# Full-height products for the last 16 tokens, and one triangle product instead of two, in a two-layer hybrid kernel

## The chip, the cores and the metric

The kernel runs on one core of a Trainium2 chip. The metric is the device time of one execution in microseconds. Engines are named as in the profile: PE is the matrix engine (TensorE), PEld its weight loads, DVE the vector engine, ACT the scalar engine, POOL GpSimd, SP the engine that issues most transfers. "Lnnn" is a line of the kernel.

## The reference

A sequence of 256 frames, with 16 learned meta tokens ahead of it, passes two post-norm residual layers of width 2048. Layer 0 has two groups of heads behind one input projection: 4 heads of gated linear attention and 8 heads of stick-breaking attention. Layer 1 is a Mamba-2 mixer with 8 groups of 8 heads. Cut to the two parts that the change touches:

```
# layer 0, stick-breaking attention, per head (128 channels), block i of 128 queries
z         = q @ k.T                                  # keys up to the query's block
mask      = (key < query) & valid
log_stay  = where(mask, log_sigmoid(-z), 0)
within    = log_stay @ later_in_block                # strict triangle, per block of 128 keys
later     = sum of log_stay over the later key blocks
w         = where(mask, exp(log_sigmoid(z) + within + later), 0)
out       = w @ v

# layer 1, SSD scan, per head h of group g: y[t] = sum over s <= t of
#   exp(a_cum[t] - a_cum[s]) * (c[t] . b[s]) * dt[s] * x[s]   + d_skip * x[t]
```

## The kernel before

The 16 meta tokens and the 256 frames make 272 tokens, held with channels on the 128 rows and tokens along the columns. Over the tokens as rows, 272 is 128 + 128 + 16, so each token-by-token matrix comes in three blocks of keys: 128, 128 and the last 16 rows. Most of PE's work is projections: each unit of weights (128 x 2048) is loaded by SP, split by ACT (L159) and DVE or POOL (L160) into a high and a low part of type float32r, and multiplied in three passes (high by high, high by low, low by high: L178 to L180; L494 to L496 for the last projection). The token mixing of each head or group runs beside that: generators (`push`, `tick`) issue its steps between the products of the units. The order of the instructions on each engine is then laid out by the framework with a simulated timeline (`schedule_with_timeline_sim=True`); products marked with `keep_in_program_order` ("pin") stay in their own order, and the last stretches of both layers hold DVE and ACT in program order (`keep_order`).

**Layer 0, `mix_sb`.** The scores of one head lie in one bank of PSUM, `zb`, in 432 columns: 0 to 16 are the last 16 keys against the last 16 queries, 16 to 288 the first 128 keys against all 272 queries, 288 to 432 the second 128 keys against the last 144 queries. ACT, DVE and POOL make `sp` (softplus of the scores, masked) of it, and `parts_of` splits `sp` into `sph` and `spl`. The rows of the last 16 keys are copied into `sp2`, the high part into rows 0 to 15 and the low part into rows 32 to 47; the other rows of `sp2` hold zeros from the start of the kernel (L371 and L372). Then PE adds to `zb`: the negative triangle `nL_r` times both key blocks (L812 and L814), minus the sum of the second block onto the first (L816), minus the sum of the last 16 keys onto both blocks (L819: `nones_r[:48]` times `sp2`, 32 columns), and the triangle of the last 16 keys (L820: `nL2` times `sp2`, 16 columns out). ACT takes `zb` from there (L823). `sp2`, `nL2`, `sph`, `spl`, `nL_r` and `nones_r` are float32r. Here the trace calls `sph` and `spl` by their buffers, `s0h` and `s0l`.

**Layer 1, `mix_ssd`.** For a group, `M` holds the decayed token-by-token weights of 8 heads and `xd` the inputs times dt, with tokens as rows. L1257 multiplies them for the two blocks of 128 tokens; each head gives 64 rows of the output, so two heads stand side by side in the output's rows. For the last 16 tokens two heads share one product (L1263): `xd2` and `mt2` hold the one head in rows 0 to 15 and the other in rows 32 to 47, with zeros in between (memset at L936 and L937), and 32 columns, 16 for each. These tiles are plain float32; in the trace each product of that type makes two records. Both steps are pinned.

Of the kernel before, what the change touches and what calls it, by code (L numbers as in the profile page):

```python
# [6 lines left out]
F32 = mybir.dt.float32  # L7
F32R = mybir.dt.float32r
# [4 lines left out]
P = 128  # L13
# [69 lines left out]
def _wait(*tasks):  # L83
    for t in tasks:
        while not t.done:
            yield


class _Body:
# [181 lines left out]
    def layer0(self):  # L271
        nc, lp = self.nc, self.lp
# [37 lines left out]
        v2 = [lp.tile([80, 512], F32R, tag=f"v2{i}", name=f"v2{i}") for i in range(2)]  # L310
        s2 = [lp.tile([80, 1, 16], F32R, tag=f"s2{i}", name=f"s2{i}") for i in range(2)]
        self.v2, self.s2 = v2, s2
        self.sp2, self.nL2 = [lp.tile([48, n, 16], F32R, tag=t, name=t) for n, t in ((2, "sp2"), (1, "nL2"))]

        add4 = lp.tile([P, 432], F32, tag="ge", name="add4")[:, :P]

# [467 lines left out]
    def mix_sb(self, h, q, k, v):  # L784
        nc, lp = self.nc, self.lp
        act, vec, mm = nc.scalar.activation, nc.vector, nc.tensor.matmul
        zb = self.zbank()
        gk = dict(skip_group_check=True)

        for a, b in ((0, 0), (0, 1), (1, 0)):  # L790
            mm(zb[:, 16:288], k[:, a, 0:128], q[:, b, :], start=a == b, stop=False, **gk)
        for a, b in ((0, 0), (0, 1), (1, 0)):
            mm(zb[:, 288:432], k[:, a, 128:256], q[:, b, 128:T], start=False, stop=False, **gk)
        for a, b in ((0, 0), (0, 1), (1, 0)):
            mm(zb[:16, 0:16], k[:, a, 256:T], q[:, b, 256:T], start=False, stop=False, **gk)
        yield

        sp = e = lp.tile([P, 432], F32, tag="ge", name=self.nm("sbe"))
        act(e, zb[:, :432], AF.Abs)
        act(e, e, AF.Exp, scale=-1.0)  # L800
        act(e, e, AF.Ln, bias=self.b_one)
        vec.scalar_tensor_tensor(sp[:, :432], zb[:, :432], 0.0, e, op0=ALU.max, op1=ALU.add)
        yield
        self.causal(sp[:16, 0:16], 16, True)
        self.causal(sp[:, 16:144], 128, True)
        self.causal(sp[:, 288:416], 128, True)
        yield
        sph, spl = self.parts_of(sp, self.sp2, (0, 1))
        yield

        for s in (sph, spl):
            mm(zb[:, 16:288], self.nL_r, s[:, 16:288], start=False, stop=False, **gk)  # L812
        for s in (sph, spl):
            mm(zb[:, 288:432], self.nL_r, s[:, 288:432], start=False, stop=False, **gk)  # L814
        for s in (sph, spl):
            mm(zb[:, 144:288], self.nones_r, s[:, 288:432], start=False, stop=False, **gk)  # L816

        last = zb[:, 144:432].rearrange("p (a c) -> p a c", a=2)[:, :, 128:144]
        mm(last, self.nones_r[:48, :], self.sp2, start=False, stop=False, **gk)  # L819
        mm(zb[:16, 0:16], self.nL2[:, 0, :], self.sp2[:, 0, :], start=False, stop=True, **gk)  # L820
        yield
        w = self.spad
        act(w, zb[:, :432], AF.Exp)  # L823
        self.causal(w[:, 16:144], 128, True)
        self.causal(w[:, 288:416], 128, True)
        self.causal(w[:16, 0:16], 16, True)
        yield
        s2 = self.s2[h % 2]
        wh, wl = self.parts_of(w, s2, (0, 0, 1))
        yield  # L830
        while ("sv", h) not in self.tasks:
            yield
        yield from _wait(self.tasks["sv", h], self.tasks["sr", h // 4])
        o = self.po()
        self.values(o, *v, slice(0, P), wh, wl, s2)
        yield
        j, g = h % 4, 4 + h // 4
        mh, ml = self.mix_tile(g) if j == 0 else self.mix[g]
        y = lp.tile([P, T], F32, tag="gs2", name=self.nm("sby"), bufs=2)
        vec.tensor_tensor(y, o[:, :T], self.cur["sr", h // 4][:, j, :], op=ALU.mult)  # L840
        act(mh[:, j, :], y, AF.Copy)
        vec.tensor_tensor(ml[:, j, :], y, mh[:, j, :].bitcast(F32), op=ALU.subtract)
        yield
# [83 lines left out]
    def layer1(self):  # L927
        nc, lp = self.nc, self.lp
        self.acc = lp.tile([P, 2, D], F32, tag="acc", name="acc")
        self.y0 = self.y_tiles()  # L930
        self.mt = lp.tile([16, HPG, 16], F32, tag="mt", name="mt")


        self.mt2 = lp.tile([48, 4, 2, 16], F32, tag="mt2", name="mt2")
        self.xd2 = lp.tile([48, 4, 64], F32, tag="xd2", name="xd2")
        nc.vector.memset(self.mt2, 0.0)  # L936
        nc.vector.memset(self.xd2, 0.0)  # L937
        self.xq = lp.tile([P, 4, 32], F32, tag="xq", name="xq")
        nc.vector.memset(self.xq, 0.0)
        self.rstd1 = {}  # L940
        self.first1()
        self.units(len(L0), L1[:-5], {n: None for n in range(NFIRST)})
        self.tail()
# [537 lines left out]
```

## Time and profile before

| what | value |
|---|---|
| median of 3 runs | 1380.34 us (1380.31 to 1380.48) |
| profiled execution | 1380.1 us |
| its span, first to last instruction | 1378.4 us |
| PE busy | 1369.2 us (99%) |
| DVE busy | 1033.7 us (75%) |
| ACT busy | 770.1 us (56%) |
| POOL busy | 261.7 us (19%) |
| share of the 16 DMA engines, main queue | 53.8% |
| granted PE clock over the span | 0.999 |
| stick-breaking heads, L812 to L820 | 438 to 631 us of the span |
| groups of layer 1, L1257 and L1263 | 776 to 1309 us of the span |

Products are pipelined: the duration of one in the trace is from its start to a modelled end, and the next one starts before that. So PE's pace is read from start to start. A form such as "48*128 48x32" is weights of 48 rows by 128 columns and a moving operand of 48 rows by 32 columns; float32r stands as f32 in the forms of PE.

### The profile page before, as it was taken

To read this page: it belongs to the slowest core of one execution; us is meant where nothing else is said; L and a number is where in the kernel's file an instruction comes from. 1 tells how busy PE (TensorE), PEld (TensorE's weight loads), DVE (VectorE), ACT (ScalarE), POOL (GpSimd) and SP (SyncE) were. 2 spreads that over 40 slices of the span, in tenths; PEclk is the share of its full clock that TensorE was granted. 3 is DMA by queue.
4 is the path that set the end of the run, shared out by engine and by line. 5 is a ranking of instruction groups with operands and counts; after the bars stand their busy time and mean duration, and the time that the engine had idled before them with its cause. 6 is when DMAs were issued, how large, how long until landed. Compare 5 with 4: busy or idle time off the path is not lost.

```text
span 1378.4 us, 26195 instructions
## 1 busy us (share of the span) xinstructions
PE 1369.2 (99%) x10619; PEld 1319.5 (96%) x10619; DVE 1033.7 (75%) x1763; ACT 770.1 (56%) x1149; POOL 261.7 (19%) x253
## 2 busy tenths in 40 slices
PE   9999999999999999999999999999999999999998
PEld 8999999999999999999999999899898999989986
DVE  7858576576565574568899999887877879777687
ACT  6646455355345554556587677656565655656551
POOL 0000010100101100004500143331322323133221
PEclk9999999999999999999999999999999999999999
DMA  9656446446445455554455655565555555555561
GB/s 333 207 173 200 166 162 209 160 163 217 168 158 188 139 192 167 196 168 136 136 196 170 240 203 203 177 240 184 210 176 202 185 200 217 172 194 186 183 214 62
DMA packets 61945, 256.73 MB, mean 186 GB/s; under 512 B 26176, under 2 KB 29056, under 8 KB 33408
## 3 DMA queue, kind: packets, MB, share of 16 engines
q1 hardware_dynamic: 61104, 254.27, 53.8%
q8 instruction: 83, 1.36, 0.4%
q10 hardware_dynamic: 720, 0.79, 0.2%
q14 instruction: 38, 0.31, 0.1%
HBM read 249.29 MB, written 5.74 MB: 185 GB/s over the span
## 4 chain that ended last, share of the span: by engine, by line
PE 92%; DVE 5%; issue 1%; DMA 1%; POOL 0%; ACT 0%; SPq 0%; ACTq 0%; DVEq 0%; POOLq 0%
PE pj L178 25%; PE pj L179 25%; PE pj L180 25%; PE pj L494 4%; PE pj L496 4%; PE pj L495 4%; PE po L1257 1%; PE po L631 1%; DVE wlo L160 1%; DVE M L1127 1%; DMA raw<-in_wts 0%; PE po L1196 0%; DVE M L1128 0%; DVE M L1155 0%; DVE xt L1072 0%
## 5 line engine op out<-in xcount | busy, mean ns | idle before, releaser
L178 PE MATMUL pj<-xhi,whi 128*128 128x272 f32 (+4 forms) x2560 | 731.6, 286 | 1.5 <-ACT xhi L330 0.6
L179 PE MATMUL pj<-xlo,whi 128*128 128x272 f32 (+4 forms) x2560 | 730.4, 286 | 0.0
L180 PE MATMUL pj<-xhi,wlo 128*128 128x272 f32 (+4 forms) x2560 | 729.7, 285 | 0.0
L159 ACT ACTIVATE whi<-raw 128x1024 fp32r<-128x1024 f32 (+2 forms) x434 | 449.2, 1038 | 384.0 <-PE pj L179 312.3
L160 DVE TENSOR_TENSOR wlo<-raw,whi 128x1024 fp32r<-128x1024 f32 (+2 forms) x405 | 503.1, 1247 | 200.4 <-ACT whi L159 192.6
L178 PEld LDWEIGHTS pj<-xhi,whi 128*128 128x128 f32 x2560 | 482.0, 188 | 3.7 <-ACT whi L159 1.3
L179 PEld LDWEIGHTS pj<-xlo,whi 128*128 128x128 f32 x2560 | 482.0, 188 | 1.7 <-issue 1.0
L180 PEld LDWEIGHTS pj<-xhi,wlo 128*128 128x128 f32 x2560 | 482.1, 188 | 0.4 <-issue 0.4
L178 PE MATMUL pj<-mixh,whi 128*128 128x272 f32 x384 | 110.7, 290 | 0.0
L180 PE MATMUL pj<-mixh,wlo 128*128 128x272 f32 x384 | 110.5, 288 | 0.0
L179 PE MATMUL pj<-mixl,whi 128*128 128x272 f32 x384 | 110.4, 288 | 0.0
L160 POOL TENSOR_TENSOR wlo<-raw,whi 128x1024 fp32r<-128x1024 f32 x29 | 73.1, 2522 | 191.2 <-ACT whi L159 176.7
L494 PE MATMUL pj<-whi,yh 128*128 128x512 f32 (+1 forms) x240 | 93.3, 389 | 0.0
L495 PE MATMUL pj<-wlo,yh 128*128 128x512 f32 (+1 forms) x240 | 92.6, 386 | 0.0
L496 PE MATMUL pj<-whi,yl 128*128 128x512 f32 (+1 forms) x240 | 92.2, 386 | 0.0
L261 POOL TENSOR_TENSOR gr<-gr,gsc 128x1088 f32<-128x1088 f32 x6 | 15.4, 2575 | 303.1 <-ACT gsc L260 303.1
L179 PEld LDWEIGHTS pj<-mixl,whi 128*128 128x128 f32 x384 | 72.3, 188 | 0.2
L180 PEld LDWEIGHTS pj<-mixh,wlo 128*128 128x128 f32 x384 | 72.3, 188 | 0.0
L178 PEld LDWEIGHTS pj<-mixh,whi 128*128 128x128 f32 x384 | 72.2, 188 | 0.2
L503 DVE SCALAR_TENSOR_TENSOR acc<-pj,rr,acc 128x512 f32<-128x512 f32 (+1 forms) x65 | 46.5, 734 | 13.9 <-PE pj L496 13.7
L496 PEld LDWEIGHTS pj<-whi,yl 128*128 128x128 f32 x240 | 45.1, 188 | 9.2
L494 PEld LDWEIGHTS pj<-whi,yh 128*128 128x128 f32 x240 | 45.1, 188 | 8.9
(349 smaller groups left out, 1460.5 us busy)
## 6 DMA issues: line engine op xcount, KB each, us to landing
raw<-in_wts SPq DMA_DIRECT2D x212, 1024.0 KB, 4.9
ebc<-edr SPq DMA_DIRECT2D x8, 1664.0 KB, 6.5
raw<-in_wts SPq DMA_DIRECT2D x9, 256.0 KB, 5.4
vdr<-vt SPq DMA_DIRECT2D x8, 256.0 KB, 4.8
vt<-vdr SPq DMA_DIRECT2D x32, 64.0 KB, 2.4
hacc<-in_xT SPq DMA_DIRECT2D x7, 272.0 KB, 6.1
early<-in_wts SPq DMA_DIRECT2D x2, 512.0 KB, 7.1
vdr<-vt SPq DMA_DIRECT2D x8, 128.0 KB, 3.5
```

The lines of the kernel that those rows point to most:

```text
L159: self.nc.scalar.activation(hi, src, AF.Copy)
L160: eng.tensor_tensor(lo, src, hi.bitcast(F32), op=ALU.subtract)
L178: mm(ps, whi, xhi, start=first, stop=False)
L179: mm(ps, whi, xlo, start=False, stop=False)
L180: mm(ps, wlo, xhi, start=False, stop=last)
L261: mul(c, c, e, op=ALU.mult)
L494: mm(ps, yh[:, kk, tt], hi[:, k, :], start=kk == 0, stop=False)
L495: mm(ps, yh[:, kk, tt], lo[:, k, :], start=False, stop=False)
L496: mm(ps, yl[:, kk, tt], hi[:, k, :], start=False, stop=kk == 3)
L503: self.nc.vector.scalar_tensor_tensor(a, ps, r[:, t : t + 1], a, op0=ALU.mult, op1=ALU.add)
L631: mm = lambda r, a, b, start=False, stop=False: self.nc.tensor.matmul(o[:, r], a, b, start=start, stop=stop, skip_group_check=True)
L1127: vec.tensor_scalar(M[:, h, 0:256], eb[:, h, 0:256], self.est[:, 0, 0, gh : gh + 1], 0.0, op0=ALU.subtract, op1=ALU.min)
```

## The change

The tiles with the last 16 tokens get 128 rows instead of 48, so that the zeros go on to row 127 and the products over them contract over 128 rows. The instructions that fill them are the same, with more rows. L812 takes both key blocks at once, columns 16 to 432, and the two products of L814 are gone.

```diff
@@ layer0
-        self.sp2, self.nL2 = [lp.tile([48, n, 16], F32R, tag=t, name=t) for n, t in ((2, "sp2"), (1, "nL2"))]
+        self.sp2, self.nL2 = [lp.tile([P, n, 16], F32R, tag=t, name=t) for n, t in ((2, "sp2"), (1, "nL2"))]
@@ mix_sb
         for s in (sph, spl):
-            mm(zb[:, 16:288], self.nL_r, s[:, 16:288], start=False, stop=False, **gk)
-        for s in (sph, spl):
-            mm(zb[:, 288:432], self.nL_r, s[:, 288:432], start=False, stop=False, **gk)
+            mm(zb[:, 16:432], self.nL_r, s[:, 16:432], start=False, stop=False, **gk)
         for s in (sph, spl):
             mm(zb[:, 144:288], self.nones_r, s[:, 288:432], start=False, stop=False, **gk)
 
         last = zb[:, 144:432].rearrange("p (a c) -> p a c", a=2)[:, :, 128:144]
-        mm(last, self.nones_r[:48, :], self.sp2, start=False, stop=False, **gk)
+        mm(last, self.nones_r, self.sp2, start=False, stop=False, **gk)
         mm(zb[:16, 0:16], self.nL2[:, 0, :], self.sp2[:, 0, :], start=False, stop=True, **gk)
@@ layer1
-        self.mt2 = lp.tile([48, 4, 2, 16], F32, tag="mt2", name="mt2")
-        self.xd2 = lp.tile([48, 4, 64], F32, tag="xd2", name="xd2")
+        self.mt2 = lp.tile([P, 4, 2, 16], F32, tag="mt2", name="mt2")
+        self.xd2 = lp.tile([P, 4, 64], F32, tag="xd2", name="xd2")
```

The line numbers behind the change are two lower from L814 on.

## The prediction

> **What bounds the kernel now.** First the head of the page and its chain line.
>
> ```profile
> span 1378.4 us, 26195 instructions
> ...
> PE 92%; DVE 5%; issue 1%; DMA 1%; POOL 0%; ACT 0%; SPq 0%; ACTq 0%; DVEq 0%; POOLq 0%
> ```
>
> The chain of work that ended last is TensorE for 92%, so a product that goes away counts unless something is late right behind it. Since the change has two places, one in layer 0 and one in layer 1, I next asked for the busy time by stretches (columns: stretch, length, then PE, weight load, DVE, ACT, POOL, granted clock, DMA).
>
> ```profile
> 420.00:722.00 302.00, 302.00 (x2438) 300.58 (x2437) 209.78 (x357) 168.19 (x275) 49.54 (x77) 1.00 0.51 169
> 722.00:842.00 120.00, 118.57 (x995) 113.48 (x994) 117.63 (x227) 86.83 (x138) 33.63 (x27) 1.00 0.58 209
> 842.00:1330.00 488.00, 488.00 (x3635) 457.65 (x3634) 378.41 (x587) 287.54 (x409) 138.14 (x104) 1.00 0.55 194
> ```
>
> The reader sees three regimes. From 420 to 722 (the stick-breaking heads and the end of layer 0) TensorE is never idle. From 842 to 1330 (layer 1, groups 2 to 7) neither. Between them, VectorE is busy 117.63 of 120 and TensorE idles 1.43: there VectorE holds part of the chain. The waits and the chain of that stretch name the place:
>
> ```profile
> PE pj L178 <- DVE fix L958: 0.5, 1, 0.5
> ...
> 722.42 0.45 PE po L1012 x4
> 722.93 0.43 DVE xlo L984
> ...
> 724.10 1.14 DVE wlo L160
> ```
>
> Up to 722.42 the chain is TensorE's own, and VectorE's run from 722.93 starts off it. So time taken out of TensorE in layer 0 moves that run forward with it. A busy TensorE still says nothing of how fast it streams, so from here I read distances between starts of products, in the timeline of TensorE (columns: start, duration, then the instruction; the durations overlap).
>
> **The stick-breaking heads.** One head of eight:
>
> ```profile
> 438.27 0.29 PE L812 MATMUL z<-s0h,nL 128*128 128x272 f32 x1
> 438.40 0.29 PE L179 MATMUL pj<-xlo,whi 128*128 128x272 f32 x1
> ...
> 439.52 0.29 PE L812 MATMUL z<-s0l,nL 128*128 128x272 f32 x1
> 439.64 0.23 PE L814 MATMUL z<-s0h,nL 128*128 128x144 f32 x1
> 439.71 0.28 PE L814 MATMUL z<-s0l,nL 128*128 128x144 f32 x1
> 439.82 0.28 PE L816 MATMUL z<-s0h,nones 128*128 128x144 f32 x1
> 439.93 0.28 PE L816 MATMUL z<-s0l,nones 128*128 128x144 f32 x1
> 440.14 0.28 PE L819 MATMUL z<-sp,nones 48*128 48x32 f32 x1
> 440.27 0.17 PE L820 MATMUL z<-sp,nL 48*16 48x16 f32 x1
> 440.37 0.39 PE L179 MATMUL pj<-xlo,whi 128*128 128x272 f32 x1
> 440.60 0.29 PE L180 MATMUL pj<-xhi,wlo 128*128 128x272 f32 x1
> ```
>
> A product of 272 columns takes 0.124 from start to start (nine dense ones between 438.40 and 439.52). One of 144 takes 0.11 in a row of its kind, where its weights are the limit, and 0.07 where a longer product before it covered the weights (439.64 to 439.71). Ahead of the first 48-row product there are 0.21 instead of 0.11, behind it 0.13, and the first dense product after the 48-row pair takes 0.23. From L812 with s0l to L180 that is 1.08 us.
>
> After the change: two products of 416 columns replace four. A 512-column product gives the slope:
>
> ```profile
> 879.62 0.39 PE L496 MATMUL pj<-whi,yl 128*128 128x512 f32 x1
> ...
> 880.53 0.39 PE L494 MATMUL pj<-whi,yh 128*128 128x512 f32 x1
> ```
>
> Four starts in 0.91 are 0.228 each; with 0.124 at 272 columns that is 0.43 ns a column, so 416 columns take 0.186. For the last 16 tokens, L819 becomes 128*128 with 32 columns, a full-height load like its neighbours: 0.11 ahead of it, bounded by 0.07 below and 0.21 above; I take 0.11, since the load that paces L816 is the same. L820 becomes 128*16. The trace has such products in two kinds. The tiles here (sp2, nL2) are float32r, as at L795:
>
> ```profile
> 429.97 0.28 PE L793 MATMUL z<-qe,ke 128*128 128x144 f32 x1
> 430.08 0.22 PE L795 MATMUL z<-qe,ke 128*16 128x16 f32 x3
> 430.16 0.37 PE L180 MATMUL pj<-xhi,wlo 128*128 128x272 f32 x1
> 430.37 0.29 PE L178 MATMUL pj<-xhi,whi 128*128 128x272 f32 x1
> ```
>
> 0.11 into it, 0.027 for each, and 0.21 for the dense product behind. The plain float32 kind at L717 costs more:
>
> ```profile
> 86.25 0.29 PE L715 MATMUL z<-gq,gk 128*128 128x144 f32 x1
> 86.47 0.27 PE L717 MATMUL z<-gq,gk 128*16 128x16 f32 x4
> 86.66 0.39 PE L179 MATMUL pj<-xlo,whi 128*128 128x272 f32 x1
> 86.89 0.29 PE L180 MATMUL pj<-xhi,wlo 128*128 128x272 f32 x1
> ```
>
> 0.22 into it (0.10 more), and behind it 0.23 after a last step that leaves about 0.08 more than L795's. So L820 costs between nothing and 0.2 a head above L795's figures; I take L795's, whose type and shape are the same.
>
> The new run from L812 with s0l: 0.186 to L816, 0.07 (weights covered by the long product), 0.11 to L819, 0.11 to L820, 0.03 to the dense product, 0.21 to the next: 0.716 against 1.08, 0.364 less. The s0h product, which runs alone earlier among dense ones, grows from 0.13 to 0.186: 0.06 back. Net 0.30 a head, eight heads: **2.4 us**. In 420 to 722 nothing else holds TensorE, so all of it is on the path. No wait is added: the 416-column product needs the same s0h or s0l that the 272-column one needed, on the same queue.
>
> The Trainium skill, "TensorE: Matmul & The Clock Gate", section "Back-to-back issue gap", gives N/2.4 + 2.5 ns when warm, 176 ns for 416 columns. By it the sum would be 0.16 us larger. The 272-column rows do not follow it (116 ns by the formula, 124 here), so the rows decide.
>
> **The groups of layer 1.** L1257 and L1263 work in pairs: two halves of 64 columns start together, so x2 below is one pair.
>
> ```profile
> 820.89 0.41 PE L1257 MATMUL po<-M,xd 128*64 128x144 f32 x4
> ...
> 821.02 0.29 PE L1257 MATMUL po<-M,xd 128*64 128x144 f32 x2
> 821.24 0.42 PE L1263 MATMUL po<-mt,xd 48*64 48x32 f32 x8
> ...
> 821.38 0.28 PE L1263 MATMUL po<-mt,xd 48*64 48x32 f32 x4
> ...
> 821.43 0.23 PE L1263 MATMUL po<-mt,xd 48*64 48x32 f32 x2
> 821.59 0.39 PE L178 MATMUL pj<-xhi,whi 128*128 128x260 f32 x1
> ```
>
> Pairs of L1257 come 0.12 apart; from the last of them to L1263 there are 0.22, so 0.10 is the price of going from 128*64 to 48*64. Of L1263's four pairs (821.24, 821.32, 821.38, 821.43 from these rows) the first takes 0.08 and the others 0.06. With 128 rows the shape stays 128*64: 0.10 goes at the border and 0.02 of the first pair, whose weights load beside L1257; at most that whole pair's load, 0.06, goes. The way out to 128*128 stays as it is, since 64 columns remain. That is 0.12 to 0.16 a group; I take 0.13.
>
> ```profile
> L1263 PE MATMUL po<-mt,xd x64: 219/219/240, 785.4 to 1308.6; 48*64 48x32 f32 x64
> ...
> 785.15 0.29 PE L180 MATMUL pj<-xhi,wlo 128*128 128x272 f32 x1
> ```
>
> Eight records a group make eight groups. In the first (785.4) a dense product stands ahead of L1263, so nothing goes there. Seven groups by 0.13: **0.9 us**. One of them, at 821, lies in the stretch where VectorE is full; its 0.13 may be lost. The range for the layer is 0.7 to 1.1.
>
> **The fills** of the taller tiles cost nothing: 80 and 48 rows take the same time (start, duration),
>
> ```profile
> 5.12 0.16 DVE L372 TENSOR_SCALAR s<-nones_f 80x16 fp32r<-80x16 f32 x1
> ...
> 5.28 0.16 DVE L372 TENSOR_SCALAR nL<-nones_f 48x16 fp32r<-48x16 f32 x1
> ```
>
> and the copies that write the tiles are untouched. Without that they would cost at most the 0.16 again, four times, once.
>
> **Sum.** 2.4 + 0.9 = 3.3 us. The profiled execution took 1380.1, its span 1378.4 and 1.7 around it; it becomes 1376.8, the span 1375.1. The median of the runs before is 1380.34, 0.24 above, so the forecast is **1377.0 us**, 0.24% less. Its own range is 1376.3 to 1377.5 (at best 0.36 a head, if the lone s0h product gives nothing back, and 1.1 in layer 1; at worst 0.27, if L819 keeps 0.03 of its 0.10, and 0.7).
>
> **The rivals.** First, the turn of shape stays at L820. 16 columns are a narrower shape than 128, as 48 rows were a lower one, and L717's rows price it at 0.2 a head, 1.6 in all: 1378.6. L795, three float32r products with no such step, speaks against it. This is also what the Trainium skill, "TensorEngine Tiling (Array Packing)", section "Key Properties", says: changing the tiling mode drains the array. By that rule a 16-column product would still drain. The rows at L819 and L1257 agree (0.21 and 0.22 where 0.11 and 0.12 are normal); the row at L795 does not (0.11).
>
> Second, layer 0's gain is hidden: TensorE comes 2.4 earlier to 722 and waits there for VectorE, which had been busy on its own account. Only layer 1's 0.9 is left: 1379.4. The chain, TensorE's until 722.42, speaks against it.
>
> Third, slower. The program's order on each engine is laid out by a simulated schedule, which sees the changed products too. If it puts more of the weight splits (L160, 1.14 each in the chain above) ahead of what TensorE waits for between 722 and 842, TensorE waits that long each time. Three of them take the whole gain; four give 1377.0 + 4.6 = 1381.6. For it: VectorE has 2.4 us free there. Against it: both places of the change lie outside, but for one group.
>
> **How the numbers follow.** Forecast 0.60; first rival 0.12; second 0.08; third 0.10; 0.10 is left for an order shuffled elsewhere, with gains up to about 4 us or down to 1. A change of 0.2% (2.76 us, below 1377.58) is about what a measurement tells from none. Faster: 0.60 and half of the rest, 0.65. Slower by over 0.2% needs six such splits: 0.03 of the third, and 0.01 of the rest: 0.04. Between: 0.31. The range from 1376.0 to 1378.9 holds the forecast, the first rival and most of the rest: 0.80.
>
> **What would show it.** No L814 and 16 products of L812 in the form 128x416; from L816 to L819 0.11; L820 in the form 128*16, 0.11 behind L819 and 0.03 ahead of the dense product, which takes 0.21; the first L1263 0.12 behind L1257. Wrong would be 0.2 at L820 (first rival), a longer wait at 723 (second), or new idle time of TensorE between 722 and 842 under other L160 rows (third).

## The result, and the profile after

| | before | after |
|---|---|---|
| median, run side by side (10 runs each) | 1380.29 us (1379.28 to 1381.42) | 1376.69 us (1376.04 to 1377.29) |
| profiled execution | 1380.1 us | 1376.89 us |
| its span | 1378.4 us | 1375.2 us |

The ratio of the times is 0.9975 with a 95% interval of 0.9967 to 0.9984. The forecast was 1377.0; the span was to become 1375.1.

The head of the page of the kernel after, then its busy time by the same stretches as before (stretch, length, PE, weight load, DVE, ACT, POOL, granted clock, DMA share, GB/s).

```profile
span 1375.2 us, 26163 instructions
```

```profile
420.00:722.00 302.00, 301.87 (x2438) 300.85 (x2436) 211.76 (x362) 170.07 (x279) 49.79 (x77) 1.00 0.51 170
722.00:842.00 120.00, 118.93 (x997) 114.37 (x997) 117.53 (x226) 86.20 (x138) 35.82 (x27) 1.00 0.59 210
842.00:1330.00 488.00, 488.00 (x3632) 458.38 (x3631) 379.68 (x588) 288.84 (x408) 138.86 (x104) 1.00 0.55 195
```

The regimes are what they were. Two numbers moved: TensorE has 0.13 us of idle time in the first stretch, where it had none, and 1.07 instead of 1.43 in the second. The first head in TensorE's timeline after (start, duration, instruction):

```profile
439.65 0.35 PE L812 MATMUL z<-s0l,nL 128*128 128x416 f32 x1
439.84 0.23 PE L814 MATMUL z<-s0h,nones 128*128 128x144 f32 x1
439.90 0.28 PE L814 MATMUL z<-s0l,nones 128*128 128x144 f32 x1
440.02 0.22 PE L817 MATMUL z<-sp,nones 128*128 128x32 f32 x1
440.09 0.17 PE L818 MATMUL z<-sp,nL 128*16 128x16 f32 x1
440.12 0.37 PE L179 MATMUL pj<-xlo,whi 128*128 128x272 f32 x1
440.32 0.29 PE L180 MATMUL pj<-xhi,wlo 128*128 128x272 f32 x1
440.45 0.29 PE L178 MATMUL pj<-xhi,whi 128*128 128x272 f32 x1
```

The 416-column product takes 0.19, the 32-column one follows 0.12 behind L814 (0.21 before), the 16-column one 0.07 behind that (0.13), and the dense product 0.03 later (0.10). From L812 with s0l to the second dense product that is 0.68 instead of 1.08. In heads 4 and 8 the planner put two dense products and one between L814 and L817; less 0.124 for each of these the sum is the same. In layer 1, the border from L1255 to L1261 in the second group (the last pair of L1255, the four pairs of L1261, the first dense product):

```profile
818.79 0.29 PE L1255 MATMUL po<-M,xd 128*64 128x144 f32 x2
...
818.91 0.38 PE L1261 MATMUL po<-mt,xd 128*64 128x32 f32 x8
...
819.00 0.29 PE L1261 MATMUL po<-mt,xd 128*64 128x32 f32 x4
...
819.22 0.39 PE L178 MATMUL pj<-xhi,whi 128*128 128x260 f32 x1
```

0.12 into L1261 instead of 0.22, and its third pair starts 0.09 behind its first, where it was 0.14: 0.15 a group. And all of L1261, first to last start:

```profile
L1261 PE MATMUL po<-mt,xd x64: 192/223/243, 783.5 to 1305.4; 128*64 128x32 f32 x64
```

The first group comes 1.9 us earlier than before (785.4), the last one 3.2 (1308.6). To see where that was won, I matched the dense products of the two traces one by one and took the difference of their starts. After against before, in us:

| from start of span | difference there | what lies behind the last point |
|---|---|---|
| 430 | +0.07 | the first loads |
| 447, 467, 487, 507 | -0.15, -0.48, -0.80, -1.15 | heads 1 to 4 |
| 587, 607, 627, 632 | -1.38, -1.70, -2.02, -2.36 | heads 5 to 8 |
| 642 | -2.06 | a wait of TensorE at 639 |
| 733 | -1.83 | dense products of 256 columns at 118 ns, not 113 |
| 848 | -2.22 | the stretch where VectorE is full, and one group |
| 1311 | -3.21 | six groups, 0.16 each |

### The profile page after: what moved, and what is told of

Its sections match the earlier page's. It is cut to its first block, busy times and chain, and to the rows that moved or that the text cites. A ratio compares the mean times of both kernels' runs of the same rounds, so it can differ in the third digit from the quotient of the medians.

```text
span 1375.2 us, 26163 instructions
## 1 busy us (share of the span) xinstructions
PE 1366.5 (99%) x10603; PEld 1318.6 (96%) x10603; DVE 1033.6 (75%) x1763; ACT 769.9 (56%) x1149; POOL 263.5 (19%) x253
## 4 chain that ended last, share of the span: by engine, by line
PE 91%; DVE 6%; issue 1%; DMA 1%; ACT 0%; POOL 0%; SPq 0%; ACTq 0%; DVEq 0%; POOLq 0%
PE pj L178 25%; PE pj L179 25%; PE pj L180 24%; PE pj L494 4%; PE pj L496 4%; PE pj L495 4%; DVE wlo L160 1%; PE po L631 1%; PE po L1255 1%; DVE M L1125 1%; DMA raw<-in_wts 0%; DVE M L1126 0%; PE po L1194 0%; DVE M L1153 0%; DVE xt L1070 0%
## 5 line engine op out<-in xcount | busy, mean ns | idle before, releaser
L178 PE MATMUL pj<-xhi,whi 128*128 128x272 f32 (+4 forms) x2560 | 732.1, 286 | 1.2 <-DVE fix L956 0.5
L178 PEld LDWEIGHTS pj<-xhi,whi 128*128 128x128 f32 x2560 | 481.9, 188 | 3.7 <-ACT whi L159 1.5
L178 PE MATMUL pj<-mixh,whi 128*128 128x272 f32 x384 | 110.9, 290 | 0.0
L178 PEld LDWEIGHTS pj<-mixh,whi 128*128 128x128 f32 x384 | 72.1, 188 | 0.4 <-ACT mixh L839 0.2
```

The source lines that it names most:

```text
L178: mm(ps, whi, xhi, start=first, stop=False)
```

## Experiments

Each line of the table below is one kernel; single runs, except where a count stands. Before the first head the starts of single traces lie up to 0.6 us away from those of before, so what decides is the distance between starts, and the matched products from 420 on.

| kernel | time, us | span |
|---|---|---|
| before, in the same sessions | 1379.6, 1380.39, 1380.27 (12 runs) | |
| merged triangle alone | 1379.73 | 1378.0 |
| tall tiles in the heads alone | 1378.71 | 1377.0 |
| tall tiles in the groups alone | 1379.9 | 1378.2 |
| all of it with 80 rows | 1377.01 | 1375.3 |
| all of it with 64 rows | 1379.95 | 1378.2 |
| 16-column product read as plain float32 | 1378.42 | 1376.7 |
| dt's splits one unit later | 1376.59 | 1374.9 |
| last values product one step later | 1375.96 | 1374.2 |
| one values product behind twelve dense ones | 1374.81 (5 runs) | 1373.3 |
| after, again | 1376.32 (8 runs) | 1374.3 |

**Which part carries it.** The theory: the turn of TensorE's shape at the 48-row products is the larger part of layer 0's gain, and the merged triangle the smaller. The rival: it is the removed products. First the triangle alone.

```diff
@@ before, mix_sb
-            mm(zb[:, 16:288], self.nL_r, s[:, 16:288], start=False, stop=False, **gk)
-        for s in (sph, spl):
-            mm(zb[:, 288:432], self.nL_r, s[:, 288:432], start=False, stop=False, **gk)
+            mm(zb[:, 16:432], self.nL_r, s[:, 16:432], start=False, stop=False, **gk)
```

> The kernel before with only the triangle merged: two products of 416 columns in place of four, the last 16 tokens still over 48 rows. Theory (the turn of shape around the 48-row products is the larger part of the heads' gain): from L812 with s0l to the 48-row product 0.46 us instead of 0.62, with 0.2 still ahead of it, less 0.065 that the lone s0h product costs more; 0.095 a head, 0.8 in all, span 1377.6. Rival (the products saved carry the heads' gain): 0.3 a head, 2.4 in all, span 1376.0.

TensorE's timeline of that kernel in the first head:

```profile
440.30 0.28 PE L814 MATMUL z<-s0l,nones 128*128 128x144 f32 x1
440.51 0.28 PE L817 MATMUL z<-sp,nones 48*128 48x32 f32 x1
440.64 0.17 PE L818 MATMUL z<-sp,nL 48*16 48x16 f32 x1
440.74 0.39 PE L179 MATMUL pj<-xlo,whi 128*128 128x272 f32 x1
```

The 0.21 ahead of the 48 rows and the 0.10 ahead of the dense product are all there. The eight heads together took 0.61 us off by the matched products (0.04 to 0.10 each), less than the 0.8 expected. So the triangle is the smaller part, and the rival falls. Next the tall tiles in the heads alone.

```diff
@@ before, layer0
-        self.sp2, self.nL2 = [lp.tile([48, n, 16], F32R, ...
+        self.sp2, self.nL2 = [lp.tile([P, n, 16], F32R, ...
@@ before, mix_sb
-        mm(last, self.nones_r[:48, :], self.sp2, start=False, stop=False, **gk)
+        mm(last, self.nones_r, self.sp2, start=False, stop=False, **gk)
```

> The kernel before with only sp2 and nL2 over 128 rows; four triangle products, layer 1 as before. Theory: from the last L816 to the second dense product 0.11 + 0.07 + 0.03 + 0.21 = 0.42 us instead of 0.66; 0.245 a head, 2.0 in all, span 1376.4, unless waits give some back as they do in the changed kernel (0.28 at 640, 0.2 at 724). Rival (products saved): 0, span 1378.4.

```profile
440.15 0.28 PE L816 MATMUL z<-s0l,nones 128*128 128x144 f32 x1
440.27 0.22 PE L819 MATMUL z<-sp,nones 128*128 128x32 f32 x1
440.34 0.17 PE L820 MATMUL z<-sp,nL 128*16 128x16 f32 x1
440.36 0.37 PE L179 MATMUL pj<-xlo,whi 128*128 128x272 f32 x1
```

0.115, 0.07 and 0.03: the turns are gone, with the triangle as it was. The heads gave 1.95, 0.24 each. With the triangle's 0.61 that is 2.56, and after measured 2.43. So the parts add up to 0.13, which goes with the pace of the dense products behind single heads (below). The time shows less of it (0.9 below before's run), since the next 46 us gave 0.79 back, for a reason that the next run has too: the tall tiles in the groups alone.

```diff
@@ before, layer1
-        self.mt2 = lp.tile([48, 4, 2, 16], F32, tag="mt2", name="mt2")
-        self.xd2 = lp.tile([48, 4, 64], F32, tag="xd2", name="xd2")
+        self.mt2 = lp.tile([P, 4, 2, 16], F32, tag="mt2", name="mt2")
+        self.xd2 = lp.tile([P, 4, 64], F32, tag="xd2", name="xd2")
```

> The kernel before with only mt2 and xd2 over 128 rows. Theory: the step from the 64-column products to those of the last 16 tokens falls from 0.22 to 0.12 us and the first pair from 0.08 to 0.03, 0.15 in each of seven groups; 1.0 in all, span 1377.4, give or take 0.3 for the stretch at 722 to 842 where VectorE is full. Rival (layer 1's share of the gain came from waits that moved because layer 0 ended earlier): the same pace at these products as before, span 1378.2 or more.

```profile
821.81 0.29 PE L1257 MATMUL po<-M,xd 128*64 128x144 f32 x2
...
821.93 0.37 PE L1263 MATMUL po<-mt,xd 128*64 128x32 f32 x8
```

By its time this run speaks for no gain at all. The trace says otherwise: 0.12 into L1263, and 0.99 us over the last six groups. What hid it lies elsewhere: 0.41 from the first loads, and 0.79 lost between 641 and 687, where the order of TensorE's instructions is the same as before's. The busy time from 645 to 670, first of before, then of this kernel:

```profile
645.00:670.00 25.00, 25.00 (x205) 25.00 (x205) 23.99 (x29) 15.15 (x30) 22.94 (x22) 1.00 0.50 168
```

```profile
645.00:670.00 25.00, 25.00 (x200) 25.00 (x199) 23.98 (x29) 15.55 (x31) 22.94 (x21) 1.00 0.48 163
```

Busy all the time in both, and at the full granted clock; yet 200 products instead of 205. The dense products of 272 columns run 126.7 ns apart there, not 123.3. I come back to that pace below. One run with a time alone would have misled here.

**How tall is tall enough.** The theory: the products must be in the same row mode as their neighbours, whatever the height that takes. The rival: any height under 128 costs. 80 rows, then 64:

```diff
@@ after, layer0, mix_sb and layer1 (sp2, nL2, mt2, xd2 alike)
-        self.sp2, self.nL2 = [lp.tile([P, n, 16], F32R, ...
+        self.sp2, self.nL2 = [lp.tile([80, n, 16], F32R, ...
-        mm(last, self.nones_r, self.sp2, ...
+        mm(last, self.nones_r[:80, :], self.sp2, ...
```

> The changed kernel with all four tiles at 80 rows instead of 128. Theory (what costs is a height that fits half of the array, 64 rows or fewer; taller weights run as full ones, as the 80-row and 96-row products elsewhere in the trace do): same as with 128 rows, 0.11 and 0.07 ahead of and behind the first product of the last tokens, 0.03 and 0.21 after, span 1375.2 give or take 0.3. Rival (any height under 128 costs): 0.2 ahead of them again, 0.25 more a head and 0.15 more a group, span 1378.2.

> The changed kernel with all four tiles at 64 rows. Theory (64 rows or fewer turn the shape): as with 48 rows; 0.2 ahead of the first product of the last tokens in each head, 0.22 from the 64-column products in each group; the merged triangle alone is left, span 1377.6. Rival (what costs is rows that end inside a 32-row strip, as 48 does): as with 128 rows, span 1375.2.

With 80 rows:

```profile
440.10 0.28 PE L814 MATMUL z<-s0l,nones 128*128 128x144 f32 x1
440.22 0.22 PE L817 MATMUL z<-sp,nones 80*128 80x32 f32 x1
440.29 0.17 PE L818 MATMUL z<-sp,nL 80*16 80x16 f32 x1
440.32 0.37 PE L179 MATMUL pj<-xlo,whi 128*128 128x272 f32 x1
```

With 64 rows, in the head and at the border of the second group:

```profile
440.45 0.28 PE L814 MATMUL z<-s0l,nones 128*128 128x144 f32 x1
440.66 0.28 PE L817 MATMUL z<-sp,nones 64*128 64x32 f32 x1
440.79 0.17 PE L818 MATMUL z<-sp,nL 64*16 64x16 f32 x1
440.89 0.39 PE L179 MATMUL pj<-xlo,whi 128*128 128x272 f32 x1
...
820.66 0.29 PE L1255 MATMUL po<-M,xd 128*64 128x144 f32 x2
...
820.88 0.42 PE L1261 MATMUL po<-mt,xd 64*64 64x32 f32 x8
```

80 rows give the distances of 128 to 0.01; 64 rows give those of 48 (0.21, 0.13, 0.10; 0.22 in layer 1), and 3.06 us more than after at the end of layer 1, of which 0.55 stood before the first head. Both rivals fall. Shown: the price is paid at 48 and 64 rows, and not at 80. The heights between 64 and 80 were not run.

**Does the 16-column product turn the shape?** That was the first rival of the prediction. The trace after says no for float32r. The same product with its tiles read as plain float32 (this changes the products' precision, and two records appear for each) tests whether the type decides, or the neighbours.

```diff
@@ after, mix_sb
-        mm(zb[:16, 0:16], self.nL2[:, 0, :], self.sp2[:, 0, :], start=False, stop=True, **gk)
+        nL2, sp2 = [a.bitcast(F32) for a in (self.nL2[:, 0, :], self.sp2[:, 0, :])]
+        mm(zb[:16, 0:16], nL2, sp2, start=False, stop=True, **gk)
```

> The changed kernel, with the operands of the 16-column triangle product (L818) read as plain float32 instead of float32r; its neighbours stay float32r. Theory (a narrow product turns the shape only in plain float32, whatever stands around it): about 0.17 into it instead of 0.07, 0.23 at the second dense product behind instead of 0.21 and a longer last step, 0.2 a head, 1.6 in all, span 1376.8. Rival (the plain products at L717 paid because their neighbours at L715 are plain too, the type does not matter): the two records cost 0.03 a head, span 1375.5.

```profile
439.82 0.22 PE L817 MATMUL z<-sp,nones 128*128 128x32 f32 x1
439.97 0.21 PE L819 MATMUL z<-sp,nL 128*16 128x16 f32 x2
440.11 0.39 PE L179 MATMUL pj<-xlo,whi 128*128 128x272 f32 x1
440.34 0.28 PE L180 MATMUL pj<-xhi,wlo 128*128 128x272 f32 x1
```

0.15 into it instead of 0.07, 0.14 to the dense product instead of 0.03, 0.23 behind that instead of 0.21: 0.2 a head, as the prediction priced the rival from L717. The time is 1.7 longer than after's; the matched products lose 2.1 over the heads, since the dense products behind some of them also ran slower (124.8 ns apart on average from 460 to 476 us, 123.9 in after). So L717's price belongs to plain float32, and L795's to float32r. The change of type alone would be another explanation, since the neighbours here are float32r. It does not hold for the way in: in after, L713, plain float32 over 128 rows and 128 columns, starts 0.13 behind a dense float32r product, and 0.12 to 0.13 is the dense products' own distance.

```profile
85.37 0.28 PE L178 MATMUL pj<-xhi,whi 128*128 128x272 f32 x1
85.50 0.62 PE L713 MATMUL z<-gq,gk 128*128 128x272 f32 x2
```

The Trainium skill, "TensorEngine Tiling (Array Packing)", section "Key Properties", says that a change of tiling mode drains the array, and its section "Available Configurations" lists modes of 64 and 32 rows, and of 64 and 32 columns. The runs agree for rows (0.10 at 48 and 64, none at 80 and 128) and for columns in plain float32; for 16 columns in float32r they do not.

**The wait at 639.** After the last head TensorE waits for ScalarE's `mixh` (L839), and that for VectorE's `sby` (L838). In the trace after, TensorE's and ScalarE's timelines (in brackets: idle before, and what ended it); the first product that reads `mixh` starts 0.29 behind the one before it instead of 0.12, and 0.06 behind `mixh`'s end:

```profile
639.33 0.28 PE L180 MATMUL pj<-mixh,wlo 128*128 128x272 f32 x1
639.62 0.77 PE L178 MATMUL pj<-mixh,whi 128*128 128x272 f32 x4
```

```profile
631.18 0.51 ACT L621 ACTIVATE gvh<-vt 128x128 fp32r<-128x128 f32 x2 [1.95 <-DMA vt<-vdr]
...
639.13 0.43 ACT L839 ACTIVATE mixh<-sby 128x272 fp32r<-128x272 f32 x1 [3.72 <-DVE sby L838]
```

The theory: the run of work up to `mixh` starts late since VectorE and ScalarE have the splits of dt's weights in that stretch; with these one unit later the wait goes.

```diff
@@ after
-        if u[2] == 5:
+        if u[2] == 6:
```

> The changed kernel, with the two splits of the dt weights (1.4 us of VectorE, at 632 to 634) made one unit later. Theory (TensorE's wait at 639.4 for the last head's mixh is VectorE's queue behind the landing of the head's v): the splits out of the way, mixh is ready 1 us sooner, the 0.28 that TensorE lost there comes back, span 1374.9. Rival (the wait is set by something else): 0.28 still lost at 639, span 1375.2.

The span came out as forecast, 1374.9, and yet nothing was tested. Timeline of ScalarE in that kernel:

```profile
630.31 0.51 ACT L621 ACTIVATE gvh<-vt 128x128 fp32r<-128x128 f32 x2 [1.65 <-DMA vt<-vdr]
630.73 0.61 ACT L159 ACTIVATE dtgvh<-dtraw 128x512 fp32r<-128x512 f32 x1
```

The planner put the split back right behind L621, where it stands in after too. There was no wait at 639: the transfer of `vt` had landed sooner, and ScalarE had waited for it 1.65 us, against 1.95 in after. Over the twelve traces of this study, a wait of 1.90 or 1.95 there goes with a wait of TensorE for `mixh` (three traces: after, 80 rows, and the values product behind twelve), and 0.87 to 1.65 with none (nine). So the wait follows a transfer whose landing differs from run to run. The transfer itself was not moved, so this is a correlation.

**The pace.** From 506 to 558 us the dense products run 126.7 ns apart in before, in after and in all the kernels above. The stretch starts behind the last values product of head 4 (L631, 80 rows by 16 columns; its tiles are 80 rows tall in every kernel). In the trace after, behind it, and the busy time of 40 us of that stretch:

```profile
505.17 0.22 PE L631 MATMUL po<-s,v 80*128 80x16 f32 x1
505.24 0.37 PE L178 MATMUL pj<-mixh,whi 128*128 128x272 f32 x1
505.45 0.29 PE L179 MATMUL pj<-mixl,whi 128*128 128x272 f32 x1
```

```profile
510.00:550.00 40.00, 40.00 (x318) 40.00 (x317) 20.54 (x24) 17.21 (x17) 2.57 (x1) 1.00 0.50 168
```

The theory: a row of short products sets the pace at which TensorE leaves it, and the pace holds until the next row; change how the row ends and the stretch is fast. The rival: the pace belongs to the stretch, to what the other engines and the transfers do there. The first try puts one step of the program between that product and the six ahead of it.

```diff
@@ after, values() takes end=True, and returns the last product if it is False
-        self.values(o, *v, slice(0, P), wh, wl, s2)
+        last = self.values(o, *v, slice(0, P), wh, wl, s2, h != 3)
+        if last:
+            yield
+            last()
```

> The changed kernel, with the last product of the values (80 rows, 16 columns) of the fourth head put some dense products later, so that it stands alone among them. In both kernels the dense products of 272 columns run at 126.7 ns from start to start from 506 to 558, and at 123.4 nearly everywhere else; the slow stretch begins behind this product where it stands in a row of short ones. Theory (which pace the dense products fall into is set by how the row of short products ahead of them ends, and holds till the next one): 415 products at 123.4, 1.4 us less, span 1373.8. Rival (the pace belongs to the work of that stretch: out-projection and mixing of heads beside it): no change, span 1375.2.

The planner put the product back in its row: it stands 0.11 behind the fifth one, as before, and the pace from 506 to 558 is still 126.7. In effect that was a second run of after (its span 1.0 us shorter: 0.4 from its first loads, 0.3 from the missing wait at 639, 0.2 from a faster stretch at 724). So the product was queued by name behind a dense product twelve further on.

```diff
@@ after, values() with hold=True keeps its last product in self.late
-        self.values(o, *v, slice(0, P), wh, wl, s2)
-        yield
+        self.late = []; self.values(o, *v, slice(0, P), wh, wl, s2, h == 3); yield
+        yield from self.issue_late()
...
+    def issue_late(self):
+        if self.late:
+            for _ in range(2):
+                yield
+            dense = next(i for i in reversed(self.traced()) if i.engine == mybir.EngineType.PE)
+            with self.tc.issue_after(dense):
+                self.late.pop()()
+            yield
```

> The changed kernel, with the last product of the values (80 rows, 16 columns) of the fourth head queued behind twelve dense products, so that it stands alone among dense ones as that of the second and third head does. Theory (the pace of the dense products is set by how the row of short products ahead of them ends, and holds until the next such row): the 415 dense products from 506 to 558 run at 123.4 ns instead of 126.7, 1.4 us less than the changed kernel, span 1373.8 where the stretches that vary from run to run fall as in its profile. Rival (the pace belongs to the work beside them in that stretch): 126.7 there still, time within 0.1% of the changed kernel.

> The changed kernel once more, on the same chip as the one with the late product. Theory: 1376.7 us, 126.7 ns from 506 to 558 as in every run so far; the stretch behind the last head's values (641 to 672) may come out at 123.4 or 126.7, as it did in runs with the same order of products, worth 0.8 us. Rival (the paces are all drawn anew in each run): 123.4 from 506 to 558 here.

The kernel with the late product, TensorE's timeline and the same 40 us:

```profile
506.25 0.29 PE L180 MATMUL pj<-mixh,wlo 128*128 128x272 f32 x1
506.37 0.18 PE L631 MATMUL po<-s,v 80*128 80x16 f32 x1
506.40 0.37 PE L178 MATMUL pj<-mixh,whi 128*128 128x272 f32 x1
506.61 0.28 PE L179 MATMUL pj<-mixl,whi 128*128 128x272 f32 x1
```

```profile
510.00:550.00 40.00, 40.00 (x326) 40.00 (x326) 21.53 (x25) 17.67 (x18) 2.57 (x1) 1.00 0.53 181
```

326 products in 40 us instead of 318, at the same granted clock: 123.3 ns apart. Against after's trace the matched products gain 1.37 us from 503 to 567, 0.12 of it at the row itself. After again has 318 products in the same 40 us, so the stretch was not drawn anew. Timed beside after again on the same chip: 1374.81 us (1374.75 to 1375.15) against 1376.32 (1375.86 to 1376.73), 1.5 less, and against before 0.9961 (0.9948 to 0.9973). This is the fastest version here. So moving this one product makes the stretch fast, and the rival falls, since the other engines' work there is the same but for one instruction or two.

That the end of a row decides in general is not shown, and two things in the traces speak against it. In after, four rows that end in the same way (the 80-row product 0.11 behind one of 144 columns, then a dense one), at 104, 175, 276 and 376 us, are followed by 123.4 to 123.6 ns. And between 641 and 672 the pace was slow in three kernels (tall tiles in the heads alone, in the groups alone, dt's splits later) and fast in the others, behind a step of 0.18 between two dense products that all have; two of the slow ones had before's very order of TensorE's instructions, the third had after's. What sets the pace is open.

## Why the prediction was right

**The heads, 2.4 forecast, 2.43 measured.** The steps: 416 columns 0.186 (0.187 to 0.191 measured), 0.07 behind it (0.066), 0.11 into L817 (0.11), 0.11 into L818 (0.07: the forecast was too large), 0.03 and 0.21 (0.026 and 0.209). The step that was off is the one into the 16-column product: I took L795's 0.11, ahead of which a product of 144 columns stands, while here one of 32 columns does. So a head is worth 0.34, not 0.30. Eight would give 2.7, but heads 1 and 5 gave only 0.23 each. Behind head 1 the rows above show why: the dense products at 440.32 and 440.45 are 0.13 apart, and they run at 126.7 ns for 4 us. Two errors of 0.3 cancelled, so that the sum came out to 0.03 is luck.

**The groups, 0.9 forecast.** 0.16 in each of the last six (0.99) and 0.15 in the second, against 0.13. Together that is 1.14, just above the forecast's own range for the layer (0.7 to 1.1). The missing 0.02 is in the first pair, which came down to 0.03 from 0.08: 0.05 of its 0.06 goes, near the bound that I had named and not taken. The first group gave nothing, as forecast.

**The fills** cost nothing that can be seen: the difference at the first head (+0.07) is within what the first loads vary (-0.5 to +0.6 over the traces).

**What I did not have.** From 632 to 848 after lost 0.30 to the wait at 639 and 0.23 to the pace at 724, and won 0.39, 0.15 of it the second group's. The rest of the 0.39 goes with TensorE's idle time in the stretch where VectorE is full, down from 1.43 to 1.07: a wait of 0.4 of TensorE for VectorE (before, L1196 for L1288) is gone. None of the eleven other traces has that wait, not even those of a part of the change alone, so that the change took it away is not shown. The two losses come and go with TensorE's instructions in the same order. After again has no wait at 639, and its matched products gain 0.30 there and 0.5 on the first loads, so its span is 1374.3; but it lost 0.22 at 724 as after did. The kernel with the last values product one step later, whose order of TensorE's instructions is after's, lost nothing at either place.

So the steps of heads and groups gave 3.57, and what lay outside them took 0.29 net. That the span came out at 1375.2 against 1375.1 is in part luck. The medians, 3.6 and 3.95 below before's, are nearer to that 3.57 than to the forecast's 3.3.

**The rivals.** The first, a turn of shape at L818, is refuted for float32r by after's own rows and confirmed in price by the plain float32 run. The second, VectorE at 722, did not come: the wait there (L178 for VectorE's L956) is 0.5 as it was. What came of that kind was the wait at 639, one step earlier, on a chain that runs from a transfer through ScalarE and VectorE to `mixh`; it costs 0.2 to 0.3 where it shows. The third, splits shuffled ahead of what TensorE waits for, did not come: TensorE's idle time there fell.

## What to carry to other kernels

Products whose weights have 48 or 64 rows, among full ones, cost about 0.1 us on the way in here, and in the heads 0.15 more up to the second dense product behind them; zeros that bring the weights to 80 rows or more take that away, and the fill cost nothing that these traces show, off the path as it is. Price each step from start to start, with the product before it, and confirm an edit by those distances and by matched products: a single time missed 0.99 us of gain in one run, and in another met its forecast without the edit having moved anything. Look at what order the planner really gave before reading any result.

## What the hardware showed that I had not expected

Dense products stream at one of two paces with the same granted clock and TensorE busy throughout: 123.4 or 126.7 ns for 272 columns, 113.3 or 117.8 for 256. The slow pace held for 415 products in the longest case, from one row of short products to the next. Of the groups of three dense products with 272 or 256 columns, 301 of 2525 were slow in after, and 161 with the one late product.
